# The first output projection of an encoder trunk: its attention rows read into the token operand, six of its tiles finished in the projections' PSUM banks, the last group's output moved inside SBUF

## The chip, the core and the metric

The kernel runs on one NeuronCore of a Trainium2 chip. TensorE (PE in the profile) multiplies and transposes, VectorE (DVE) and ScalarE (ACT) do the elementwise work and read PSUM, GpSimd (POOL) does a little elementwise work, and DMAs are issued from the queue of SyncE (SP), some from those of ACT and POOL. Every engine works through its own queue. The metric is the device time of one execution in microseconds (us); the median of several runs counts. A difference of 0.2% (5.4 us) is about the least that a measurement of this kernel tells from none.

## The reference

The kernel computes a two-layer encoder trunk on 1024 tokens of width 1024, in float32. Layer 0 mixes tokens with windowed attention (16 query heads of width 64 in four groups, each group with one key and value head, one sink per head) and four cross-attention heads into 256 memory tokens. Layer 1 has a gated linear recurrence in the place of the windowed attention. In both, the two kinds of heads are joined and go through one output projection, `y = concat(o, cross) @ w_out`, 1536 to 1024, which is normed and added to the stream; a gated convolutional feed-forward (FFN) follows.

```python
h = x
for layer in range(DEPTH):
    u = rmsnorm(h, norm_g[layer, 0])
    mem_kv = mem_n @ w_mem_kv[layer]
    ...
    y = mixer_window_attn(u, mem_kv, a_w_in[slot], a_sink[slot], a_w_out[slot], pos)   # layer 0
    ...
    h = h + rmsnorm(y, norm_g[layer, 1])
    f = conv_ffn(rmsnorm(h, norm_g[layer, 2]), ...)
    h = h + rmsnorm(f, norm_g[layer, 3])
```

```python
def mixer_window_attn(u, mem_kv, w_in, sink, w_out, pos):
    ...
    o = window_gqa_sink(q, k, v, sink).reshape(bsz, t, ATT_Q_W)
    return jnp.concatenate([o, memory_cross_attn(xq, mem_kv)], axis=-1) @ w_out
```

## The kernel before

Every operand of a large product is kept as two float32r halves, a high part and the rest (`split`, L85 to L87: a copy on ACT, a subtraction on DVE), and a product is three matmuls (`mm3`, L80 to L83: high by high, high by rest, rest by high). Tokens lie in eight tiles of 128. `uh` and `ul` are the two halves of the normed token operand, transposed: 128 partitions, eight blocks of features, 1024 tokens.

**Weights** come in units of 128 x 1024 through a staging pool of four buffers (`st`) and are split into a ring of four units (`wunit`, L68 to L78, with the load at L75, the copy at L76 and the subtraction at L77). The output projection's half needs six units; four go in the ring, two in a pool of its own (`xwh`, `xwl`).

**Layer 0's attention** (`window`) runs per group: `proj(g)` multiplies the eight token tiles by the group's query, key and value weights (`pj` in PSUM, two banks of the pool `psq`), rotates the result, transposes it (`ptq`, the third bank of `psq`) and splits it into `qs`, `kh` and `kl`. `attend(g, ...)` then goes over eight blocks of 128 queries: scores (`ps`, L315 and L316), maximum on DVE (L318), exponentials on ACT (L325), scaling, transposes of the probabilities (`pt`, L338), their split (`ph`, `pl`), and the products with the values (`po`, L341 and L342). Two blocks' outputs are gathered in `o` and stored to the DRAM buffer `oT[0]` by two DMAs on SP (L349). Cross-attention heads (`cross_unit`) are woven into groups 0 to 2 and stored to `oT[0]` rows 8 to 11 from ACT's queue (L224). `attend(g)` stands ahead of `proj(g + 1)` in the code; a scheduler that simulates the engines sets each engine's order, so that the projections of the next group fill the waits of the group before. After `proj(3)` the pool `psq` is released, and `attend(3)` has no projection beside it.

**The output projection of layer 0** was the class `WOut`. Its 12 feature blocks of 128 are read from `oT[0]` per token tile in three portions, blocks 0 to 5 (groups 0 to 2), 8 to 11 (cross heads) and 6 to 7 (group 3), each by a DMA on SP (L436) into a tile `or` that is then split. `wo0.open(3, 2)` does portions one and two of five tiles beside `attend(3)`: two of them end in SBUF (`part`), three stay in three banks of a new PSUM pool. `wo0.finish()` does the rest of the first 512 output columns (kept in `y0`, with sums of squares in `s0`), loads the second half's six units, and then does the second half, where all 12 blocks of each tile are read from DRAM and split again. Each tile's second half is followed by the norm, the addition to the stream (L493), the store to `h1d` and `norm_T` (L102 to L119), which norms again, transposes (L116) and writes `uh` and `ul` of that tile. `ffn` (matmuls at L638) then reads `uh` and `ul`.

**The class `Out`** already serves layer 1. It keeps no separate copy of the rows: `read` loads rows of `oT` into `ul` and splits them in place into `uh` and `ul`; `kept` multiplies straight from there; `cross` reads the four cross blocks of a tile into a small buffer; `begin` does blocks 0 to 5 of all eight tiles and copies each sum to `y0`; `finish` adds blocks 8 to 11 and 6 to 7, and does the second half from `uh` and `ul`.

In the profile `pb` is a PSUM bank of the output projection, `oh`, `ol` and `or` are its rows, `nu` is the row tile of `norm_T`, and `X`, `Y` and `V` are banks of the FFN.

Of the kernel before, what the change touches and what calls it, by code (L numbers as in the profile page):

```python
# [46 lines left out]
def build(tc, A, out):  # L47
# [179 lines left out]
    def window():  # L227
# [72 lines left out]
        def attend(g, qkv):  # L300
            qs, kh, kl, v = qkv
            for b in range(2):
                for nn in range(4):
# [42 lines left out]
                    if nn % 2 == 1:  # L346
# [16 lines left out]
        psq.release()  # L363
        ea.release()
        attend(3, cur)
        wo0.open(3, 2)
        psp.release()
        ap_.release()


    class WOut:

        groups = (range(0, 6), range(8, 12), range(6, 8))

        def __init__(self, l, src, key, order):
            self.l, self.src, self.key, self.order = l, src, key, order
            self.pools = [[], [], []]
            self.pre, self.part, self.begun, self.us = {}, {}, {}, {}
            self.psb, self.tag, self.psb2 = None, "pb", None

        def open(self, npre, nsb):

            l = self.l
            self.w1 = tc.alloc_tile_pool(name=f"wa{l}", bufs=2, reuse_waits="tile")
            if self.psb is None:
                self.psb = tc.alloc_tile_pool(name=f"wopb{l}", bufs=npre, space=PSUM, reuse_waits="tile")
            self.pools = [[self.w1] for _ in range(3)]
            if l == 0:

                self.w1.tile([P, 512], F32, tag="part", bufs=nsb, name="part")  # L390
                for g in (0, 2):
                    self.operands(g)
                for _ in range(2):
                    for x in ("xwh", "xwl"):
                        self.w1.tile([P, 1024], F32R, tag=x, name=x)
                self.operands(1)
            self.load(0)
            for t in self.order[npre:npre + nsb]:
                ps = self.bank()
                self.products(ps, t, 0)  # L400
                self.products(ps, t, 1, True)
                self.part[t] = self.w1.tile([P, 512], F32, tag="part", bufs=nsb, name="part")
                act.copy(self.part[t], ps)
            for t in self.order[:npre]:
                self.pre[t] = self.bank()
                for g in range(2):
                    self.products(self.pre[t], t, g)

        def bank(self):
            if self.psb2:  # L410
                return self.psb2.tile([P, 512], F32, tag="pb2", name="pb")
            return self.psb.tile([P, 512], F32, tag=self.tag, name="pb")

        def load(self, b, n=6):
            for i, u in enumerate((0, 1, 2, 4, 5, 3)[:n]):
                if (b, u) not in self.us:
                    self.us[b, u] = wunit(A[self.key][b, u], pl=self.w1 if i >= RING else None)
            self.b = b

        def products(self, ps, t, g, last=False, first=False, left=False):  # L420

            ks = [k for k in self.groups[g] if not (left and k in self.begun[t])]
            n = len(ks)
            oh, ol, raw = (x[:, :n, :] for x in self.operands(g))
            self.rows_of(ps, t, ks, oh, ol, raw, g == 0 or first, g == 2 or last)

        def operands(self, g):
            pl = self.pools[g][0]
            self.pools[g] = self.pools[g][1:] + self.pools[g][:1]
            m = len(self.groups[g])  # L430
            return [pl.tile([P, m, P], dt, tag=f"{x}{g}", bufs=1, name=x) for x, dt in (("oh", F32R), ("ol", F32R), ("or", F32))]
# [16 lines left out]
        def finish(self):  # L448
# [9 lines left out]
            for t in self.order:  # L458
# [4 lines left out]
                if t == self.order[5]:  # L463
                    after = self.read
# [1024 lines left out]
```

## Time and profile before

| | |
|---|---|
| median of 3 runs | 2690.17 us (2688.71 to 2694.2) |
| the profiled execution | 2686.47 us |
| its span, first to last instruction | 2684.7 us |
| TensorE clock granted, mean | 0.993 of full |
| busy: PE, DVE, ACT, POOL | 98%, 68%, 52%, 17% of the span |
| start of the FFN of layer 0 (first `X` product) | 595.20 us |

The profile is one execution. A row of the timeline gives start, duration, engine, line and operation, with the tile written and the tiles read, and in square brackets how long the engine had idled and for whom. A table of windows gives the busy time of each engine in each stretch, with instruction counts in brackets, then the clock that TensorE was granted as a share of full speed, and how busy the DMA engines were. Matmuls are pipelined, so one that lasts 0.39 us can start 0.23 us after another; the busy time of PE therefore overstates its work a little.

### The profile page before, as it was taken

To read this page: it belongs to the slowest core of one execution; us is meant where nothing else is said; L and a number is where in the kernel's file an instruction comes from. 1 tells how busy PE (TensorE), PEld (TensorE's weight loads), DVE (VectorE), ACT (ScalarE), POOL (GpSimd) and SP (SyncE) were. 2 spreads that over 40 slices of the span, in tenths; PEclk is the share of its full clock that TensorE was granted. 3 is DMA by queue.
4 is the path that set the end of the run, shared out by engine and by line. 5 is a ranking of instruction groups with operands and counts; after the bars stand their busy time and mean duration, and the time that the engine had idled before them with its cause. 6 is when DMAs were issued, how large, how long until landed. Compare 5 with 4: busy or idle time off the path is not lost.

```text
span 2684.7 us, 39333 instructions
## 1 busy us (share of the span) xinstructions
PE 2618.3 (98%) x14496; PEld 2200.0 (82%) x14496; DVE 1827.6 (68%) x3026; ACT 1384.6 (52%) x2530; POOL 469.4 (17%) x520
## 2 busy tenths in 40 slices
PE   8999999999999999999999999999999999999998
PEld 7888897788888887887888888888888788888886
DVE  6587787678656565478778686796757755656456
ACT  6367666645444445455455454545534444444453
POOL 1231110111111100032223132230211111110013
PEclk9999998999999999999999999999999999999999
DMA  7674213557877756674326252102436777774666
GB/s 281 213 166 104 60 28 117 176 183 181 216 199 200 205 165 243 191 241 157 103 84 177 76 120 70 48 29 83 150 119 178 183 202 210 198 205 160 220 196 228
DMA packets 204626, 427.00 MB, mean 159 GB/s; under 512 B 20112, under 2 KB 66576, under 8 KB 198800
## 3 DMA queue, kind: packets, MB, share of 16 engines
q1 hardware_dynamic: 171168, 326.68, 37.5%
q0 software_dynamic: 24544, 90.19, 16.1%
q10 hardware_dynamic: 8720, 7.60, 0.9%
q8 instruction: 114, 1.87, 0.3%
q14 instruction: 80, 0.66, 0.1%
HBM read 331.08 MB, written 117.44 MB: 167 GB/s over the span
## 4 chain that ended last, share of the span: by engine, by line
PE 77%; DVE 13%; ACT 4%; DMA 3%; issue 2%; POOL 1%; SPq 0%; DVEq 0%; ACTq 0%; POOLq 0%
PE X L638 27%; PE V L638 11%; PE pj L81 5%; PE pj L82 5%; PE Y L638 5%; PE pj L83 5%; PE pb L82 3%; PE pb L81 3%; PE pb L83 3%; DVE E L1194 1%; DVE ER L1229 1%; PE pt L338 1%; PE pt L116 1%; DVE wl L87 1%; PE po L1297 1%
## 5 line engine op out<-in xcount | busy, mean ns | idle before, releaser
L87 DVE TENSOR_TENSOR wl<-st,wh 128x1024 fp32r<-128x1024 f32 (+1 forms) x238 | 263.5, 1114 | 325.7 <-ACT wh L86 318.3
L86 ACT CAST wh<-st 128x1024 fp32r<-128x1024 f32 (+1 forms) x238 | 222.5, 937 | 295.2 <-PE X L638 196.2
L81 PE MATMUL pj<-uh,wh 128*128 128x512 f32 x512 | 204.1, 399 | 3.8 <-DVE xl L87 2.5
L638 PE MATMUL X<-wl,wh 128*128 128x512 f32 x528 | 204.8, 390 | 0.3 <-DVE wl L87 0.3
L638 PE MATMUL X<-wh,wl 128*128 128x512 f32 x528 | 204.6, 389 | 0.0
L82 PE MATMUL pj<-ul,wh 128*128 128x512 f32 x512 | 202.5, 396 | 0.1
L83 PE MATMUL pj<-uh,wl 128*128 128x512 f32 x512 | 201.6, 394 | 0.0
L638 PE MATMUL X<-wh 128*128 128x512 f32 x528 | 198.8, 390 | 1.7 <-DVE c L1014 0.9
L81 PE MATMUL pj<-wh,uh 128*128 128x384 f32 (+1 forms) x512 | 190.4, 372 | 4.2 <-DVE gs L1125 3.8
L82 PE MATMUL pj<-wl,uh 128*128 128x384 f32 (+1 forms) x512 | 187.3, 366 | 0.0
L83 PE MATMUL pj<-wh,ul 128*128 128x384 f32 (+1 forms) x512 | 186.8, 366 | 0.0
L77 DVE TENSOR_TENSOR wl<-st,wh 128x1024 fp32r<-128x1024 f32 (+1 forms) x92 | 119.9, 1310 | 28.1 <-ACT wh L76 27.4
L638 PE MATMUL V<-uh,wh 128*128 128x512 f32 x344 | 133.8, 389 | 0.0
L638 PE MATMUL V<-ul,wh 128*128 128x512 f32 x344 | 133.8, 389 | 0.0
L638 PE MATMUL V<-uh,wl 128*128 128x512 f32 x344 | 133.8, 389 | 0.0
L76 ACT CAST wh<-st 128x1024 fp32r<-128x1024 f32 (+1 forms) x99 | 99.9, 1015 | 50.5 <-PE pj L82 27.8
L638 PEld LDWEIGHTS X<-wh 128*128 128x128 f32 x528 | 99.1, 188 | 22.9 <-issue 1.3
L81 PEld LDWEIGHTS pj<-uh,wh 128*128 128x128 f32 x512 | 96.7, 189 | 24.2 <-DVE xl L87 2.9
L638 PEld LDWEIGHTS X<-wl,wh 128*128 128x128 f32 x528 | 99.1, 188 | 21.2 <-DVE wl L87 0.7
L638 PEld LDWEIGHTS X<-wh,wl 128*128 128x128 f32 x528 | 99.1, 188 | 20.8
L83 PEld LDWEIGHTS pj<-uh,wl 128*128 128x128 f32 x512 | 96.8, 189 | 19.2
L980 POOL TENSOR_TENSOR c<-c,g 128x512 f32<-128x512 f32 x24 | 43.4, 1828 | 393.8 <-PE X L638 162.8
(372 smaller groups left out, 7257.4 us busy)
## 6 DMA issues: line engine op xcount, KB each, us to landing
st<-hid SPq DMA_DIRECT2D x154, 256.0 KB, 3.1
st<-in_ffw_dram SPq DMA_DIRECT2D x108, 256.0 KB, 3.2
w2s<-in_ffw_dram POOLq DMA_DIRECT2D x24, 1024.0 KB, 7.9
st<-in_ffw_dram SPq DMA_DIRECT2D x46, 512.0 KB, 4.1
hid<-tt SPq DMA_DIRECT2D x88, 256.0 KB, 4.6
st<-w2s SPq DMA_DIRECT2D x88, 256.0 KB, 2.8
sx<-in_ffw_dram SPq DMA_DIRECT2D x84, 256.0 KB, 3.9
sy<-in_ffw_dram SPq DMA_DIRECT2D x42, 512.0 KB, 6.2
```

Source lines behind the costliest of these rows:

```text
L76: act.copy(h[:, :n], raw)
L77: (eng or dve).tensor_tensor(l[:, :n], raw, h[:, :n].bitcast(F32), op=ALU.subtract)
L81: pe.matmul(o, ah, bh, start=first, stop=False)
L82: pe.matmul(o, ah, bl, start=False, stop=False)
L83: pe.matmul(o, al, bh, start=False, stop=last)
L86: act.copy(h, src)
L87: dve.tensor_tensor(l, src, h.bitcast(F32), op=ALU.subtract)
L116: pe.transpose(ps[:, k, :], u[:, (4 * b + k) * P:(4 * b + k + 1) * P], ident)
L338: pe.transpose(tp[:, j, :], sm[:, j, c * P:(c + 1) * P], ident)
L638: pe.matmul(o, x, y, start=new, stop=e, skip_group_check=not first)
L980: pool.tensor_tensor(y[q][:, t, :], y[q][:, t, :], g3[:, c], op=ALU.mult)
L1194: dve.tensor_tensor_scan(B[:, rev], smask, a_[:, rev], 0.0, op0=ALU.mult, op1=ALU.add)
```

## The change

Layer 0's output projection uses `Out`, and `WOut` is gone. Seven things follow.

- `psq`, the three banks of the projections, is no longer released before `attend(3)`; `begin` uses its two `pj` banks and its `ptq` bank in turn.
- `begin` reads blocks 0 to 5 of each of the eight token tiles from `oT[0]` into `ul` with one DMA on SP per tile and splits them in place. A tile can be read when the store of group 2's rows has landed and the last product of `proj(3)` that reads those blocks of the tile is done. Tiles 0 and 1 have high priority.
- The first 18 matmuls of each of the eight tiles (blocks 0 to 5) then run, and ACT copies each sum to `y0`.
- In `finish` the first six tiles take the same three banks, and only tiles 6 and 7 and the second half use three more (`late`).
- For group 3, `o` goes by two DMAs on SP from SBUF to `ul`, and is split there. It is not stored to DRAM and not read back.
- The second half reads only the four cross blocks of each tile from DRAM; the other eight are taken from `uh` and `ul`.
- `y0` lies in the pool of the projection and is allocated before the last group ends.

```diff
@@ attend
-                    if nn % 2 == 1:
+                    if nn % 2 == 1 and g == 3:
+                        ts_ = slice((n - 1) * P, (n + 1) * P)
+                        oh, ol = uh[:, 6:8, ts_], ul[:, 6:8, ts_]
+                        for hp in range(2):
+                            nc.sync.dma_start(ul[hp * 64:(hp + 1) * 64, 6:8, ts_].bitcast(F32), o[:, hp::2, :])
+                        act.copy(oh, ol.bitcast(F32))
+                        dve.tensor_tensor(ol, ol.bitcast(F32), oh.bitcast(F32), op=ALU.subtract)
+                    elif nn % 2 == 1:
@@ window
-        psq.release()
         ea.release()
         attend(3, cur)
-        wo0.open(3, 2)
+        wo0.open()
+        y0 = wo0.w1.tile([P, NT, 512], F32, bufs=1, name="y0")
+        wo0.begin(psq, ("pj", "pj", "ptq"), [y0[:, t, :] for t in range(NT)])
         psp.release()
         ap_.release()
-    class WOut:
...
@@ Out.finish
-            self.banks += [(psb2, "pb2", n)] * n
+            late = [(psb2, "pb2", n)] * n
             y0 = self.y0
             s0 = wp.tile([P, NT], F32, bufs=1, name="s0")
-            for t in self.order:
+            for i, t in enumerate(self.order):
+                if i == (6, 0)[l]:
+                    self.banks += late
+                    self.used = (3, 0)[l]
                 ps = self.bank()
@@ build
-    wo0 = WOut(0, A["x"], "wout0", list(range(NT)))
+    wo0 = Out(0, A["x"], "wout0", list(range(NT)))
```

The functions of `Out` that layer 0 now calls, unchanged:

```python
def read(self, ks, c0, c1, eng):
    c = (slice(None), slice(ks[0], ks[-1] + 1), slice(c0, c1))
    raw = ul[c].bitcast(F32)
    eng.dma_start(raw, oT[self.l][ks[0]:ks[-1] + 1, :, c0:c1].rearrange("k p t -> p k t"))
    act.copy(uh[c], raw)
    dve.tensor_tensor(ul[c], raw, uh[c].bitcast(F32), op=ALU.subtract)

def begin(self, psb, tags, y0):
    ...
    for i, t in enumerate(self.order):
        if i < 2:
            with tc.high_priority(AHEAD):
                self.read(self.groups[0], t * P, (t + 1) * P, eng)
        else:
            self.read(self.groups[0], t * P, (t + 1) * P, eng)
        ps = self.bank()
        self.kept(ps, t, self.groups[0], True, True)
        act.copy(y0[t], ps)
    self.used = 0
```

How the change moves instructions shows in the order in which they stand on each engine; x2 behind a row stands for two alike in a row. First PE at the start of the last group's attention. Before, the first two products of the output projection (`pb_5277`, from `oh_5278`) stand behind scores of the group's fourth block (`ps_4875`, `ps_4879`).

```order
L315 MATMUL ps_4875<-kh_4328,qs_4472 128x384
L315 MATMUL ps_4879<-kh_4328,qs_4473 128x384
L342 MATMUL po_4699<-pl_4717,v_4330 128x512
L338 MATMUL pt_4771<-ident_74,sm_4724 128x128 x4
L316 MATMUL ps_4875<-kl_4329,qs_4472 128x384
L316 MATMUL ps_4879<-kl_4329,qs_4473 128x384
L81 MATMUL pb_5277<-wh_5241,oh_5278 128x512
L82 MATMUL pb_5277<-wl_5242,oh_5278 128x512
```

After, the first ones (`pb_5271`, straight from `uh` and `ul`) stand behind the last products of the third cross-attention head (`po_4188`, `pt_4289` is the fourth head's transposed probabilities).

```order
L83 MATMUL po_4188<-ph_4194,kvl_4118 128x512
L81 MATMUL po_4188<-ph_4206,kvh_4117 128x512
L82 MATMUL po_4188<-pl_4207,kvh_4117 128x512
L83 MATMUL po_4188<-ph_4206,kvl_4118 128x512
L217 MATMUL pt_4289<-ident_74,xp_4245 128x128 x4
L81 MATMUL pb_5271<-wh_5231,uh_78 128x512
L82 MATMUL pb_5271<-wl_5232,uh_78 128x512
L83 MATMUL pb_5271<-wh_5231,ul_79 128x512
```

So 36 products, those of tiles 0 and 1, move from the middle of the attention to the place ahead of it.

PE at the end of the last group's attention. Before, behind the last four products with the values (`po_5194`) stand six of one tile's cross rows (`pb_5560`), and then `pb_5576`.

```order
L341 MATMUL po_5194<-ph_5200,v_4330 128x512
L342 MATMUL po_5194<-pl_5201,v_4330 128x512
L341 MATMUL po_5194<-ph_5211,v_4330 128x512
L342 MATMUL po_5194<-pl_5212,v_4330 128x512
L81 MATMUL pb_5560<-xwh_5271,oh_5561 128x512
L82 MATMUL pb_5560<-xwl_5272,oh_5561 128x512
L83 MATMUL pb_5560<-xwh_5271,ol_5562 128x512
L81 MATMUL pb_5560<-xwh_5271,oh_5561 128x512
L82 MATMUL pb_5560<-xwl_5272,oh_5561 128x512
L83 MATMUL pb_5560<-xwh_5271,ol_5562 128x512
L81 MATMUL pb_5576<-xwh_5271,oh_5577 128x512
L82 MATMUL pb_5576<-xwl_5272,oh_5577 128x512
```

After, 18 products of tile 0's second half (`pb_5895`, from `uh` and `ul`) stand there, eight of tile 1's (`pb_5974`) behind them.

```order
L341 MATMUL po_5199<-ph_5205,v_4330 128x512
L342 MATMUL po_5199<-pl_5206,v_4330 128x512
L341 MATMUL po_5199<-ph_5216,v_4330 128x512
L342 MATMUL po_5199<-pl_5217,v_4330 128x512
L81 MATMUL pb_5895<-wh_5691,uh_78 128x512
L82 MATMUL pb_5895<-wl_5692,uh_78 128x512
L83 MATMUL pb_5895<-wh_5691,ul_79 128x512
L81 MATMUL pb_5895<-wh_5691,uh_78 128x512
```

The second half begins there, ahead of the first half's end, and the first product that reads group 3's rows stands 40 products behind the last `po`.

SP's queue ahead of the last group's attention. Before, three pairs of stores of group 2's rows (L349) stand together, the weight loads (L75) behind them, and the first read of rows (`or_5280`) last.

```order
L349 DMA oT0_57<-o_3504 64x2x256 x2
L349 DMA oT0_57<-o_3837 64x2x256 x2
L349 DMA oT0_57<-o_3982 64x2x256 x2
L75 DMA st_5267<-in_wout0_dram 128x1024
L75 DMA st_5273<-in_wout0_dram 128x1024
L75 DMA st_5776<-in_wout0_dram 128x1024
L75 DMA st_5782<-in_wout0_dram 128x1024
L436 DMA or_5280<-oT0_57 128x6x128
```

After, the reads of rows into `ul_79` (L401) stand two by two between the stores, which are L356 now.

```order
L401 DMA ul_79<-oT0_57 128x6x128 x2
L356 DMA oT0_57<-o_3504 64x2x256 x2
L401 DMA ul_79<-oT0_57 128x6x128 x2
L356 DMA oT0_57<-o_3837 64x2x256 x2
L401 DMA ul_79<-oT0_57 128x6x128 x2
L75 DMA st_5257<-in_wout0_dram 128x1024
L75 DMA st_5263<-in_wout0_dram 128x1024
L356 DMA oT0_57<-o_3982 64x2x256 x2
L75 DMA st_5693<-in_wout0_dram 128x1024
L401 DMA ul_79<-oT0_57 128x6x128 x2
```

The last pair of stores (`o_3982`) has moved behind a pair of reads and two weight loads, and the reads of tiles 6 and 7 stand behind it.

ACT's queue at the same place. Before, it goes from the copies of projection and cross-attention results (`v_4330`, `xo_4301`, `qs_4637`) to the first exponentials (L325) of group 3.

```order
L279 CAST v_4330<-pj_4598 128x64
L223 COPY xo_4301<-po_4276 128x512
L294 CAST qs_4637<-ptq_4632 64x512
L224 DMA oT0_57<-xo_4301 128x512
L296 CAST qs_4638<-ptq_4632 64x512
L325 ACTIVATE sm_4664,su_4668<-sm_4664,nm_4666 128x256 x4
```

After, the casts of tiles 6 and 7's rows (`uh_78` from `ul_79`, L402) stand among them.

```order
L279 CAST v_4330<-pj_4598 128x64
L402 CAST uh_78<-ul_79 128x6x128
L294 CAST qs_4637<-ptq_4632 64x512
L402 CAST uh_78<-ul_79 128x6x128
L223 COPY xo_4301<-po_4276 128x512
L325 ACTIVATE sm_4663,su_4667<-sm_4663,nm_4665 128x256 x4
```

The first exponentials stand behind both casts. The six casts of tiles 0 to 5 stand further ahead, among the copies of `proj(3)`; on DVE the eight subtractions (L403) stand in the same way, those of tiles 6 and 7 right behind the maximum of group 3's first block.

117 lines of the change are left out of this document (removed).

## The prediction

> **What bounds the kernel now.** I read the page's totals first, then busy time by stretch around the last group's attention, then PE's waits there.
>
> ```profile
> span 2684.7 us, 39333 instructions
> PE 2618.3 (98%) x14496; PEld 2200.0 (82%) x14496; DVE 1827.6 (68%) x3026; ACT 1384.6 (52%) x2530; POOL 469.4 (17%) x520
> ```
>
> PE carries the time, and the change neither adds nor removes a matmul. So it can win only time in which PE does less than it could, or lose by making PE wait where it does not. The profiled execution took 2686.47 us, 1.8 above its span and 3.7 below the median of the runs; I take a difference worked out on the span over to the median as it is. A difference under 0.2% (5.4 us) is what a measurement of this kernel can't tell from none.
>
> A row of the next table has a stretch's length, the busy time of PE, PEld, DVE, ACT and POOL, the granted clock, the DMA engines' share and GB/s.
>
> ```profile
> 360.00:400.00 40.00, 39.65 (x252) 37.92 (x251) 31.33 (x86) 28.08 (x78) 4.68 (x8) 1.00 0.05 14
> 400.00:410.00 10.00, 8.05 (x46) 6.41 (x45) 9.88 (x21) 6.06 (x10) 4.10 (x4) 0.99 0.72 213
> 410.00:420.00 10.00, 8.56 (x28) 6.24 (x28) 9.19 (x34) 8.49 (x28) 0.00 (x0) 0.50 0.47 141
> 420.00:430.00 10.00, 8.19 (x28) 5.77 (x28) 8.06 (x17) 9.69 (x20) 0.00 (x0) 0.65 0.24 69
> 430.00:480.00 50.00, 50.00 (x254) 42.27 (x253) 33.40 (x90) 31.50 (x78) 0.00 (x0) 1.00 0.35 98
> 480.00:490.00 10.00, 9.21 (x50) 7.34 (x50) 6.96 (x14) 6.48 (x15) 0.00 (x0) 1.00 0.29 73
> 490.00:500.00 10.00, 6.74 (x31) 5.05 (x30) 4.22 (x7) 5.10 (x11) 0.00 (x0) 1.00 0.37 97
> 540.00:590.00 50.00, 50.00 (x246) 41.94 (x245) 38.73 (x69) 26.71 (x53) 6.04 (x11) 1.00 0.58 184
> 590.00:600.00 10.00, 9.01 (x44) 7.18 (x44) 8.11 (x15) 4.20 (x8) 1.65 (x3) 1.00 0.50 179
> ```
>
> Three places are short of work: the start of group 3's attention (400 to 430), its tail (480 to 500) and the end of the norm (590 to 600). Counting busy time times clock as work, 400 to 430 lost 10 - 8.05 x 0.99 = 2.0, 10 - 8.56 x 0.50 = 5.7 and 10 - 8.19 x 0.65 = 4.7, together 12.4 us; 480 to 500 lost 0.8 + 3.3 = 4.1, the norm's end 1.0. The ceiling is about 17.5 us. A product that moves into these stretches saves its length; one that moves elsewhere saves nothing.
>
> **The start: 36 products moved ahead.** The maxima on DVE and the exponentials on ACT hold PE up, and no product of the projection is ready.
>
> ```profile
> PE ps L315 <- DVE mx L318: 2.8, 4, 1.2
> 410.69 0.61 DVE L318 CUSTOM_DVE_ANT_0 sm<-ps,wmask,sk 128x384 f32<-128x384 f32 x1
> 411.22 0.51 ACT L325 ACTIVATE sm<-sm,nm 128x256 f32<-128x256 f32 x1
> 417.56 1.91 PE L338 MATMUL pt<-ident,sm 128*128 128x128 f32 x8
> 426.95 0.39 PE L81 MATMUL pb<-wh,oh 128*128 128x512 f32 x1
> 429.61 0.50 PE L83 MATMUL pb<-wh,ol 128*128 128x512 f32 x1 [0.26 <-DVE ol L87]
> 607.42 2.72 PE X L638 x12
> ```
>
> The first row is a group of waits (sum, count, longest). The last, from the chain, gives a 128x512 product at full clock: 2.72 / 12 = 0.227 us. Before, the first product of the output projection ran at 426.95, and from 429.61 they ran without waits. Now 36 stand ahead of the attention; two had run before 429.61 in any case, so 34 x 0.227 = 7.7 us of work moves from the full stretch into the hole.
>
> Against it stands that on ACT the first exponentials, and on DVE the second block's maximum, now wait behind the reads of tiles 6 and 7. Their chain by rows:
>
> ```profile
> 398.69 1.23 SPq L349 DMA_DIRECT2D oT<-o  x2
> 403.65 0.33 SPq L75 DMA_DIRECT2D st<-in_wout_dram  x1
> 409.28 0.39 SPq L436 DMA_DIRECT2D or<-oT  x1
> oT<-o SPq DMA_DIRECT2D x12, 128.0 KB, 2.4
> or<-oT SPq DMA_DIRECT2D x16, 384.0 KB, 3.7
> DMA to landing us min/median/max: 2.1/3.4/8.5
> 425.69 0.84 ACT L86 CAST oh<-or 128x768 fp32r<-128x768 f32 x1
> 537.10 0.95 DVE L87 TENSOR_TENSOR ol<-or,oh 128x768 fp32r<-128x768 f32 x1
> ```
>
> The last store of group 2 went at 398.69 before. It now stands behind two weight loads, the second of which went at 403.65, so it goes at 404.0; its second half, 0.6 later, lands 2.4 after that, at 407.0. The two reads follow, 0.39 apart, and land 3.7 later, at 410.7 and 411.1. Two casts of 0.84 end at 412.4, the subtractions of 0.95 at 413.4. The exponentials start at about 413, 1.8 later than 411.22. Of that 0.84 comes back, since the cast at 425.69 is out of the way by then, but the second maximum is delayed by more than the first exponentials; I take 1.4 for the start of the dense run. Four score products of some 0.17 that were done by then are not: 0.7. Net 7.7 - 1.4 - 0.7 = **5.6 us gained**. Bounds: reads that land after 8.5 instead of 3.7 take 4.8 of it and leave about 1; with the clock at full, what can be won rises to 12.4 less these 2.1, about 10. I take 5.6, as the median landing is that of the same shape.
>
> The clock stood at 0.50 and 0.65 although none of the waits for a maximum was longer than 1.2 us. The Trainium skill, "TensorE: Matmul & The Clock Gate", section "HAM oscillation — how this bites in real kernels", says that gaps of PE under some 3.4 us keep the clock up; by that rule only waits were lost here, and with the same products moved the sum would be the same. The trace disagrees, and the measurement decides.
>
> **The tail.**
>
> ```profile
> 482.03 0.50 PE L341 MATMUL po<-ph,v 128*128 128x512 f32 x1 [0.34 <-DVE o L345]
> 486.84 0.50 PE L81 MATMUL pb<-xwh,oh 128*128 128x512 f32 x1 [0.44 <-ACT oh L86]
> 491.04 0.40 ACT L86 CAST oh<-or 128x256 fp32r<-128x256 f32 x1 [0.58 <-DMA or<-oT]
> 491.46 0.58 ACT L344 COPY o<-po 64x512 f32<-64x512 f32 x1
> 492.08 0.68 DVE L345 TENSOR_TENSOR o<-po,o 64x512 f32<-64x512 f32 x1 [0.18 <-ACT o L344]
> 492.82 0.50 PE L341 MATMUL po<-ph,v 128*128 128x512 f32 x1 [2.09 <-DVE o L345]
> 496.58 0.50 PE L81 MATMUL pb<-xwh,oh 128*128 128x512 f32 x1 [1.17 <-ACT oh L86]
> ```
>
> The square brackets say how long PE stood and for whom: 0.34 + 0.44 + 2.09 + 1.17 = 4.0 us. The two waits for `oh` (1.6) go, since the products there now read rows that have long been split. The two for `o` (a bank of `po` that must be emptied) stay in part: the cast of read rows at 491.04, 0.40, no longer stands ahead of the copy of `o`, and eight products stand ahead of the last block where six did, 2 x 0.227; I take 0.9. **2.5 us gained**, between 0 (other waits take their place) and 4.0. Group 3's rows no longer go to DRAM and back: after `o`'s 0.58 and 0.68 come two issues (1.23, as at 398.69), 2.4 to land, a cast like that copy (0.58) and a subtraction (0.68), 6.2 us. The 40 products that stand ahead of the first one that needs them cover 40 x 0.227 = 9.1. If that cover were gone, the whole 6.2 would show. The casts wait for these moves in ACT's and DVE's queues, and behind the last of them there is nothing urgent but `y`. Behind the last moves on SP stand gains of the norm and rows of the stream, wanted some 40 us later, and the reads of the second half.
>
> **The end of the norm.**
>
> ```profile
> 594.38 1.06 PE L116 MATMUL pt<-ident,nu 128*128 128x128 f32 x8 [0.99 <-DVE nu L112]
> 595.20 0.48 PE L638 MATMUL X<-uh,xwh 128*128 128x512 f32 x1
> ```
>
> PE waited 0.99 for the last tile's norm. Now 24 products of `X` and 24 of `Y`, 10.9 us, stand ahead of the last two tiles' transposes. **1.0 gained**, between 0 and 1.0.
>
> **Six more reads in group 2's attention.** The casts and subtractions of tiles 0 to 5 move into the stretch before 400, where PE was busy for 39.65 of 40. They bring 6 x 0.84 = 5.0 to ACT's 28.08 and 6 x 0.95 = 5.7 to DVE's 31.33, which is then at 37 of 40, as busy as in 410 to 420, where PE did 8.56 of 10. Bounds 0 and 4 x (10 - 8.56) = 5.8 us. I take a quarter, **1.4 lost**: the products of `proj(3)`, which need neither engine, stand there to fill waits.
>
> **At nothing.** The second half reads 4 of 12 blocks again where it read 12; PE is busy for 50.00 of 50 between 540 and 590, so fewer reads there free DMA, ACT and DVE but no time. The weights of the second half are split earlier, beside the attention, where DVE had 33.40 of 50. Eight copies to `y0` take the place of two to `part` and six to `y0`. The three banks of `late` are free long before tile 6 wants them.
>
> Sum: 5.6 + 2.5 + 1.0 - 1.4 = 7.7 us; 2690.2 - 7.7 = **2682.5** (the profiled execution 2678.8).
>
> **The rivals.**
>
> Slower, by the queues (R1). The reads of tiles 0 to 5 wait for a store, a product of `proj(3)` and a landing; their casts stand in ACT's queue ahead of the copies that empty `pj`. If the landing isn't covered, PE stops.
>
> ```profile
> 408.80 0.59 ACT L223 COPY xo<-po 128x512 f32<-128x512 f32 x1 [2.27 <-DMA oT<-xo]
> 409.29 0.58 ACT L294 CAST qs<-ptq 64x512 fp32r<-64x512 f32 x1
> ```
>
> Here ACT stood 2.27 us for a DMA with a cast of `qs` behind it. The Trainium skill, "PSUM — Partial Sum Buffer", section "Engine vs sequencer instructions", says that the queues of ScalarE and VectorE are strictly in order; this trace agrees. Price: 3.7 for the landing less 0.4 for one instruction ahead, 3.3 x 6 = 20 us against gains of 9.1: slower by 11, 2701. It decides from (9.1 + 5.4) / 6 = 2.4 us per read on PE's path. Against it: two `pj` banks and the attention's products stand between.
>
> No difference (R2). Between 400 and 420 DVE was busy for 9.88 and 9.19 of 10. If it sets the pace, two more subtractions and late landings push all of group 3 back: the start yields its lower bound, 1, the tail the 1.6, the norm 1.0, less 1.4: 2.2, or 2688.
>
> More (R3). The 36 products stand in one row before the hole and could keep the clock at full. The start then reaches half way to its upper bound (+2.2), the tail all of its 4.0 (+1.5), the reads cost nothing (+1.4): 12.8, or 2677.4. The Trainium skill, "TensorE: Matmul & The Clock Gate", section "What's actually happening", has the clock return after a busy stretch of some 3.4 us, which speaks for it; whether it would stay there no run here shows.
>
> That the change doesn't do what it says is settled by the order: ahead of the attention's last `po`, 270 products of the projection stand where 168 did.
>
> **Chances.** My forecast 0.50, with its own range 2677 to 2687, of which four parts in five lie below 2684.8; R3 0.16; R2 0.16; R1 0.18, as the queues' waits are what the trace of before shows least. Faster: 0.40 + 0.16 = 0.56; same: 0.10 + 0.16 = 0.26; slower: 0.18. The range, 2673 to 2692, reaches past R3 by the rest of the ceiling and past R2 by as much as a run's spread; it leaves out most of R1 and little below.
>
> **What would show it.** Right: PE near full and the clock near 1.00 in the first part of 400 to 430, the first exponentials near 413, no waits for `oh` at the tail, the first `X` product 7.7 us earlier than its 595.20. Wrong: PE waits of over 2 us for copies of `pj` (L279) or a lower PE share before 400 (R1); first exponentials after 416 or a clock that stays at 0.5 until 430 (R2).

## The result, and the profile after

The changed kernel takes 2678.70 us (median of 5 runs, 2677.03 to 2679.18), the kernel before beside it 2690.74 (2688.71 to 2694.2): a ratio of 0.9953, 95% interval 0.9939 to 0.9968, or 12 us. The profiled execution took 2679.18 us with a span of 2677.4.

The page's totals of the changed kernel, and the table of stretches with the columns that were explained above:

```profile
span 2677.4 us, 39198 instructions
...
PE 2614.8 (98%) x14496; PEld 2198.1 (82%) x14496; DVE 1817.4 (68%) x3012; ACT 1374.8 (51%) x2510; POOL 476.8 (18%) x520
```

```profile
360.00:400.00 40.00, 39.05 (x241) 36.82 (x242) 33.65 (x91) 29.03 (x78) 3.45 (x6) 1.00 0.19 54
400.00:410.00 10.00, 9.09 (x56) 8.04 (x55) 8.99 (x15) 7.97 (x12) 4.26 (x4) 1.00 0.55 134
410.00:420.00 10.00, 10.00 (x48) 8.20 (x46) 6.61 (x16) 4.83 (x13) 2.39 (x2) 1.00 0.74 234
420.00:430.00 10.00, 8.09 (x35) 5.95 (x34) 9.07 (x29) 7.41 (x19) 0.00 (x0) 0.83 0.27 79
430.00:480.00 50.00, 49.76 (x247) 42.09 (x247) 34.92 (x91) 37.32 (x88) 0.00 (x0) 1.00 0.23 69
480.00:490.00 10.00, 10.00 (x54) 8.39 (x53) 5.66 (x15) 4.73 (x8) 0.00 (x0) 1.00 0.39 105
490.00:500.00 10.00, 10.00 (x53) 8.26 (x52) 6.60 (x15) 5.79 (x17) 0.00 (x0) 1.00 0.10 29
580.00:590.00 10.00, 9.06 (x44) 7.32 (x43) 7.75 (x14) 3.97 (x9) 2.27 (x3) 1.00 0.48 163
```

Between 410 and 420, where PE stood at half clock, it is now full at clock 1.00. Of the hole at the start there remains 420 to 430, at 0.83. The tail at 480 to 500 is full. Two things got worse: 360 to 400 has lost 0.6 us of PE, and the end of the norm still has its gap, now at 580 to 590.

Busy time overstates PE's work, so the comparisons below use a finer count. The time between the starts of successive matmuls, less what the first of them takes at full clock when they run back to back (0.227 us for 512 columns, 0.174 for 384, 0.116 for 256, 0.109 for a transpose), is called *lost*, and is summed over a stretch of the trace. It holds waits and low clock together. A row is good to some tenths of a microsecond; the expectations below go by a coarser count of the same kind, up to 0.5 lower. The second traces are further executions of the same two kernels.

| lost by PE, us | 340 to 400 | 400 to 440 | 440 to 480 | 480 to 520 | 520 to 610 | together |
|---|---|---|---|---|---|---|
| before | 2.1 | 15.0 | 0.5 | 5.3 | 1.5 | 24.3 |
| before, second trace | 2.2 | 15.3 | 0.5 | 5.3 | 1.4 | 24.7 |
| changed | 5.2 | 7.2 | 0.5 | 1.2 | 1.7 | 15.7 |
| changed, second trace | 5.3 | 7.6 | 0.5 | 1.3 | 1.6 | 16.2 |

So the start gave 7.8 us (forecast 5.6), the tail 4.1 (2.5), the norm's end nothing (1.0), and the last group but one cost 3.1 (1.4): together 8.6 by the first traces and 8.5 by the second, where the forecast had 7.7. The rest of the 12 lies behind this part of the kernel, and is the subject of the last experiments.

Times in a trace count from its first instruction, and executions stand up to 3.8 us apart before this part begins. The first rotation of group 3's projection on POOL (L276) tells by how much; where the text counts from there, it says "from the rotation".

| us from the first instruction | that rotation | first exponentials of group 3 | first `X` product |
|---|---|---|---|
| before | 345.25 | 411.22 | 595.20 |
| changed | 345.13 | 417.90 | 585.35 |
| without the 36 products ahead | 343.78 | 416.49 | 591.99 |
| before, hole filled | 346.50 | 414.43 | 600.85 |
| group 3's rows through DRAM | 343.54 | 416.21 | 589.00 |
| weight loads behind the store | 347.33 | 415.82 | 587.40 |
| splits of six tiles left out | 346.50 | 414.75 | 585.34 |
| splits of tiles 2 to 7 behind | 345.17 | 414.36 | 588.74 |
| last tile's bank | 343.77 | 416.48 | 582.87 |

In the changed kernel one more tile's transposes stand behind the first `X` product, 0.9 us; the same instructions of the feed-forward come 9.0 us earlier than before.

The start of group 3's attention in the changed kernel:

```profile
406.35 0.67 DVE L345 TENSOR_TENSOR o<-po,o 64x512 f32<-64x512 f32 x1
407.05 1.23 SPq L356 DMA_DIRECT2D oT<-o  x2
410.15 1.26 SPq L401 DMA_DIRECT2D ul<-oT  x2
415.05 0.83 ACT L402 CAST uh<-ul 128x768 fp32r<-128x768 f32 x1 [4.71 <-DMA ul<-oT]
417.90 0.51 ACT L325 ACTIVATE sm<-sm,nm 128x256 f32<-128x256 f32 x1
421.46 0.63 PE L286 MATMUL ptq<-ident,rq 128*128 128x128 f32 x4 [1.34 <-DVE qs L297]
421.54 0.62 DVE L318 CUSTOM_DVE_ANT_0 sm<-ps,wmask,sk 128x384 f32<-128x384 f32 x1
431.05 0.39 PE L81 MATMUL pb<-wh,uh 128*128 128x512 f32 x1
```

The last store of group 2 went at 407.05, right behind group 2's last output (L345), and not at 404.0. The reads went at 410.15, and ACT stood 4.71 us for the landing. In the chain of work that ended last, this landing is one step:

```profile
410.64 6.03 DMA ul<-oT
```

So it took 6.0 us where the forecast had 3.7. The first exponentials came at 417.90, five later than forecast, and the next block's maximum at 421.54. Yet the products run on from 431.05, as forecast: the 36 products covered most of this wait.

### The profile page after: what moved, and what is told of

Its sections match the earlier page's. It is cut to its first block, busy times and chain, and to the rows that moved or that the text cites. A ratio compares the mean times of both kernels' runs of the same rounds, so it can differ in the third digit from the quotient of the medians.

```text
span 2677.4 us, 39198 instructions
## 1 busy us (share of the span) xinstructions
PE 2614.8 (98%) x14496; PEld 2198.1 (82%) x14496; DVE 1817.4 (68%) x3012; ACT 1374.8 (51%) x2510; POOL 476.8 (18%) x520
## 3 DMA queue, kind: packets, MB, share of 16 engines
q0 software_dynamic: 24544, 90.19, 16.2%
## 4 chain that ended last, share of the span: by engine, by line
PE 76%; DVE 13%; DMA 4%; ACT 3%; issue 2%; POOL 1%; SPq 0%; ACTq 0%; DVEq 0%; POOLq 0%
PE X L508 27%; PE V L508 11%; PE pj L81 5%; PE Y L508 5%; PE pj L82 5%; PE pj L83 5%; PE pb L82 3%; PE pb L81 3%; PE pb L83 3%; DVE E L1064 1%; PE pt L338 1%; DVE ER L1099 1%; DVE wl L87 1%; DVE wl L77 1%; PE pt L116 1%
```

## The experiments

Each kernel ran beside the kernel before on the same chip. Where an expectation names the changed kernel, 2678.7 is meant; a second set of runs of it gave 2678.47 (2677.98 to 2679.98).

**Without the 36 products ahead.** In layer 0, all products of the first part stand behind the first block's products with the values (`mark['pe']` is the last of these).

```diff
-                self.kept(ps, t, self.groups[0], True, True)
+                if self.l == 0:
+                    with tc.issue_after(mark['pe'].ins):
+                        self.kept(ps, t, self.groups[0], True, True)
...
```

> The changed kernel, but the products of the projection stand behind the first block's products with the values, as they did before the change; the reads stay where they are. Theory (the 36 products fill the hole at the start): their 7 to 8 us come back, 2685 to 2688, with PE at about 14 us lost between 400 and 440 and the granted clock at 0.5 to 0.7 there again. Rival (the gain is the tail's, the start is bound by the maxima and exponentials whatever stands ahead): 2678 to 2681.

Measured: 2691.02 us (2684.68 to 2692.60), ratio 1.0000 (0.9991 to 1.0009). All of the gain is gone, which is more than the theory's 7 to 8. The trace is that of the fastest of the eleven executions.

```profile
410.00:420.00 10.00, 7.35 (x23) 5.27 (x24) 9.24 (x29) 5.83 (x15) 1.26 (x2) 0.61 0.78 257
420.00:430.00 10.00, 7.74 (x28) 5.89 (x27) 7.86 (x23) 9.93 (x28) 0.00 (x0) 0.71 0.12 31
```

The hole is back at clocks of 0.61 and 0.71, and 400 to 440 loses 14.9 us, 7.7 more than in the changed kernel. The tail keeps its gain (0.4 lost in 480 to 520, against 5.3 before), but 340 to 400 loses 5.2 as in the changed kernel, and 520 to 610 loses 4.1 against 1.5:

```profile
591.99 0.50 PE L514 MATMUL X<-uh,xwh 128*128 128x512 f32 x1 [2.04 <-DVE y L494]
...
594.22 0.63 PE L514 MATMUL X<-ul,xwh 128*128 128x512 f32 x1
594.65 0.63 PE L514 MATMUL X<-uh,xwl 128*128 128x512 f32 x1
```

The first `X` waits longer here for the bank that `y` has to leave, and behind that wait products start 0.43 us apart instead of 0.227. Against before, 4.9 are won and 3.1 and 2.6 lost: without the 36 products the other parts of the change come to nothing. Against the changed kernel these stretches give 9.3 of the 12.3 us: 7.7 is the hole, as the theory has it, and 2.4 is the wait at the end, which the edit brought with it, less 0.8 won at the tail.

**Filling the hole of the kernel before with other products.**

```diff
+        for r in range(2):
+            ps = psq.tile([P, 384], F32, tag="pj", bufs=2, name="pj")
+            for k in range(24):
+                pe.matmul(ps, uh[:, k % KT, :P], ul[:, (k + 1) % KT, :384], start=k == 0, stop=k == 23)
         psq.release()
```

> The kernel before, with 48 extra products of 128x384 (48 x 0.174 = 8.4 us of PE at full clock) that need nothing but the token operand, ahead of the last group's attention; their result is used nowhere. Theory (the hole is empty of work, and the products that fill it cost nothing of their own): within 2 us of before, 2689 to 2693. If half of the loss there is the low clock and a filled PE keeps the clock up: 3 to 5 us faster than before, 2685.5 to 2688. Rival (the time at the start is PE's own at a low clock, so that extra products add to it): 8 us slower, 2699.

Measured: 2696.95 us, ratio 1.0027 (1.0018 to 1.0036): 7.3 slower, near the rival.

```profile
410.00:420.00 10.00, 9.96 (x61) 9.11 (x59) 6.07 (x21) 6.16 (x17) 0.00 (x0) 1.00 0.51 164
420.00:430.00 10.00, 5.94 (x20) 2.90 (x19) 9.50 (x24) 8.29 (x23) 0.00 (x0) 0.92 0.03 13
...
414.43 0.51 ACT L325 ACTIVATE sm<-sm,nm 128x256 f32<-128x256 f32 x1
```

The clock did come up, to 1.00 and 0.92, and still the hole was not free. 400 to 440 lost 10.2 instead of 15.0, so 4.8 of the 8.4 us were hidden and 3.6 were paid there. From the rotation, the extra products push the first exponentials by 2.0 us (67.9 for 66.0), and the hole moves behind them with the group's own chain of maxima, exponentials and transposes. From the rotation, the feed-forward began 4.4 us later than before (254.4 for 250.0); the rest of the 7.3 lies in the later stages. So the rival's reason (PE's own time at a low clock) is not what this shows either: with the clock up, PE still waits for the chain. In the changed kernel the exponentials are late too, and it wins because its products are work that otherwise stands behind.

**Group 3's rows through DRAM again.**

```diff
-                    if nn % 2 == 1 and g == 3:
+                    if nn % 2 == 1 and g == 4:
...
+                if l == 0:
+                    self.read(self.groups[2], t * P, (t + 1) * P, nc.sync)
                 self.cross(ps, t, True, False)
```

> The changed kernel, with group 3's rows stored to DRAM and read back tile by tile. Theory (40 products of 0.227 = 9.1 us stand ahead of the first that needs them; store and read back take 0.58 + 0.68 + 1.23 + 2.4 + 0.39 + 2.5 + 0.4 + 0.43 = 8.6): nothing to 1 us slower than the changed kernel, 2678 to 2680. Rival (the move inside SBUF is what took the tail's waits away): the tail's 4 to 5 us come back, 2683 to 2684.

Measured: 2681.24 us (2680.55 to 2682.76), ratio 0.9965 (0.9953 to 0.9978): 2.5 to 2.8 slower than the changed kernel, between the two expectations.

```profile
489.87 0.50 PE L81 MATMUL pb<-xwh,uh 128*128 128x512 f32 x1 [1.27 <-ACT uh L402]
...
507.09 0.50 PE L81 MATMUL pb<-xwh,uh 128*128 128x512 f32 x1 [1.61 <-ACT uh L402]
```

The waits for rows read back return, and 480 to 520 loses 6.1 where the changed kernel loses 1.2; behind the second wait, products start 0.43 us apart until 511. In the changed kernel one wait for the moved rows is left:

```profile
504.34 0.62 ACT L351 CAST uh<-ul 128x512 fp32r<-128x512 f32 x1 [0.62 <-DMA ul<-o]
505.01 0.50 PE L81 MATMUL pb<-xwh,uh 128*128 128x512 f32 x1 [0.55 <-ACT uh L351]
509.26 0.39 PE L342 MATMUL po<-pl,v 128*128 128x512 f32 x1
510.30 0.68 DVE L345 TENSOR_TENSOR o<-po,o 64x512 f32<-64x512 f32 x1 [0.72 <-ACT o L344]
514.14 0.62 ACT L351 CAST uh<-ul 128x512 fp32r<-128x512 f32 x1 [3.87 <-DMA ul<-o]
514.79 0.69 DVE L352 TENSOR_TENSOR ul<-ul,uh 128x512 fp32r<-128x512 f32 x1 [3.81 <-ACT uh L351]
518.56 0.39 PE L81 MATMUL pb<-xwh,uh 128*128 128x512 f32 x1
```

The rows that PE waits for at 505.01 are those of the third pair of blocks, whose first reader stands ahead of the last block's products with the values (509.26). The last pair's rows, for which the 40 products were counted, are split by 515.5, 5.8 us behind the end of the last product with the values, and first read at 518.56: that cover was long enough, with 3 us to spare. So it is in this experiment: the two waits belong to the second and the third pair, and the last pair costs none, as the theory has it. What the theory left out are the earlier pairs, which have less cover. By the medians the move inside SBUF is worth 2.5 to 2.8 us, most of what the tail gained.

**The weight loads behind the last store.**

```diff
-            self.load(0, self.w1)
+            if self.l == 0:
+                self.load(0, self.w1, 1)
+                with tc.issue_after(mark['sp'].ins):
+                    self.load(0, self.w1)
...
```

> The changed kernel, with the weight loads of the projection behind the last store of group 2 on SP instead of ahead of it. The reads of tiles 6 and 7, issued at 410.15 in the changed kernel, then go some 6 to 8 us earlier, and the first exponentials, at 417.9, start at 411 to 412. Theory (the late landing costs the start what the forecast's lower bound says, up to 4.8): 2 to 5 us faster than the changed kernel, 2674 to 2677. Rival (the 36 products cover the wait, and later weights cost as much): 2678 to 2680.

Measured: 2677.59 us (2676.96 to 2679.28), ratio 0.9952 (0.9939 to 0.9964): not to be told from the changed kernel.

```profile
407.68 1.23 SPq L356 DMA_DIRECT2D oT<-o  x2
409.01 1.97 SPq L75 DMA_DIRECT2D st<-in_wout_dram  x4
411.15 1.07 SPq L403 DMA_DIRECT2D ul<-oT  x2
415.82 0.50 ACT L325 ACTIVATE sm<-sm,nm 128x256 f32<-128x256 f32 x1
```

From the rotation, the store went 1.6 us earlier and the reads 1.2, not 6 to 8. The store does not wait for the loads ahead of it, but for group 2's last output, which comes at 406.35 in the changed kernel and came 8 us earlier before:

```profile
397.98 0.68 DVE L345 TENSOR_TENSOR o<-po,o 64x512 f32<-64x512 f32 x1 [0.53 <-ACT o L344]
```

Yet from the rotation the first exponentials came 4.3 us earlier than in the changed kernel (68.5 for 72.8), because the casts of tiles 6 and 7 now stand behind them, so the edit does tell what the late exponentials cost. 400 to 440 loses 5.7 instead of 7.2, 480 to 520 loses 2.5 instead of 1.2, and the feed-forward begins as far from the rotation as in the changed kernel (240.1 and 240.2). So the rival is nearer: the 36 products cover most of the wait, and what little the earlier exponentials give is lost again at the tail.

**The casts and subtractions of six tiles left out.** The rows of tiles 0 to 5 are read, but not split.

```diff
+            if self.l == 0 and c0 < 6 * P:
+                return
             act.copy(uh[c], raw)
             dve.tensor_tensor(ul[c], raw, uh[c].bitcast(F32), op=ALU.subtract)
```

> The changed kernel without the casts and subtractions of tiles 0 to 5 (their rows are loaded into the operand, but not split). Theory (casts and subtractions on ACT and DVE are what costs the last group but one its time, 4.7 us lost between 340 and 400 against 2.0 before): the 2.8 us come back there, the stretch loses 2 to 2.5, and the whole is 2 to 4 us faster than the changed kernel, 2674.5 to 2676.5. Rival (the loss there is the order's or the transfers'): 4 to 5 us lost there as before, 2677.5 to 2679.

Measured: 2676.5 us (2674.99 to 2680.74), ratio 0.9949 (0.9936 to 0.9963), which four runs can't tell from the changed kernel. 340 to 400 loses 2.1, as before the change: the theory's place is right. But 480 to 520 loses 2.9, so of the 3.1 us saved ahead 1.7 are lost again at the tail; from the rotation, the feed-forward begins 1.4 us earlier than in the changed kernel (238.8 for 240.2).

What the splits do there is seen around 357. The changed kernel, with the rotation's addition on POOL, the subtraction of tile 1's rows on DVE, and the transposes of the rotated rows on PE:

```profile
356.91 1.95 POOL L276 TENSOR_TENSOR rq<-t,t 128x320 f32<-128x320 f32 x1 [10.63 <-DVE t L275]
...
357.20 0.94 DVE L403 TENSOR_TENSOR ul<-ul,uh 128x768 fp32r<-128x768 f32 x1
...
358.92 0.33 PE L286 MATMUL ptq<-ident,rq 128*128 128x128 f32 x1 [0.97 <-POOL rq L276]
```

The same addition before, and in the kernel without the splits:

```profile
356.70 0.86 POOL L276 TENSOR_TENSOR rq<-t,t 128x320 f32<-128x320 f32 x1 [10.30 <-DVE t L275]
```

```profile
358.01 0.86 POOL L276 TENSOR_TENSOR rq<-t,t 128x320 f32<-128x320 f32 x1 [10.37 <-DVE t L275]
```

Beside the subtraction the addition takes 1.95 us instead of 0.86, 1.09 more, and PE waits 0.97 for it. The Trainium skill, "SBUF — State Buffer", section "Who interferes with whom", says that a VectorE instruction with two inputs in SBUF and a GpSimd instruction that reads SBUF exclude each other at a shared port; the trace agrees, in that the added 1.09 is about the subtraction's 0.94. It was the addition, begun 0.29 us ahead, that took longer; the subtraction took no more than that shape takes elsewhere (0.95 in the kernel before). The other losses between 340 and 400 are waits of 0.3 to 0.5 for `pl`, which stands behind the subtractions on DVE.

**The splits of tiles 2 to 7 behind the first exponentials.** The edit names the whole reads and the last of these exponentials (`mark['act']`); in the run only the casts and subtractions moved.

```diff
+                elif self.l == 0 and i >= 2:
+                    with tc.issue_after(mark['act'].ins):
+                        self.read(self.groups[0], t * P, (t + 1) * P, eng)
```

> The changed kernel with the reads of tiles 2 to 7 behind the exponentials of group 3's first block; tiles 0 and 1 stay where they are. Theory (reads ahead cost 2.8 us before 400, and those of tiles 6 and 7 hold the first exponentials back from 411 to 418): the first exponentials at 411 to 414, but six casts and subtractions (5.0 and 5.7 us) then lie in the hole; net 0 to 3 us faster than the changed kernel, 2675.5 to 2679. Rival (in the hole ACT and DVE set the pace, so that work there costs all its length): 2 to 6 us slower, 2681 to 2685.

Measured: 2681.69 us (2680.96 to 2682.03), ratio 0.9965 (0.9953 to 0.9978): 3 slower than the changed kernel, the rival.

```profile
356.97 1.96 POOL L276 TENSOR_TENSOR rq<-t,t 128x320 f32<-128x320 f32 x1 [10.66 <-DVE t L275]
```

The transfers of tiles 2 to 5 still went before 400, by SP's queue; only tiles 0 and 1 are split there, and the loss is 5.2, the same as with six. So the cost ahead is not so much per read, nor is it the transfers': the first two splits make all of it, 1.1 of the 3.1 by the clash at 357. The four splits of tiles 2 to 5 cost nothing that shows where they were; in the hole they cost, 8.8 against 7.2 in 400 to 440 and 3.0 against 1.2 in 480 to 520. The first exponentials come at 414.36, 3.5 us earlier than in the changed kernel, and the whole is slower all the same.

**The last tile's bank.**

```diff
+            self.used += 1 if l == 0 else 0
             for t in self.order:
                 pool.tensor_tensor(y0[t], y0[t], g1[:, :512], op=ALU.mult)
```

> The changed kernel with the second half's banks taken one further on, so that the last tile does not use the bank that the first product of X gets. Theory (the first X waits 0.94 us for the last tile's y to leave its bank): that wait goes, 0.5 to 1 us faster, 2677.7 to 2678.2. Rival (the wait passes to another bank or to the norm): 2678.4 to 2679.

Measured: 2678.07 us (2676.15 to 2678.52), ratio 0.9953 (0.9940 to 0.9967). The first product of `X` in the changed kernel, and here:

```profile
585.35 0.50 PE L508 MATMUL X<-uh,xwh 128*128 128x512 f32 x1 [0.94 <-DVE y L488]
```

```profile
582.87 0.48 PE L509 MATMUL X<-uh,xwh 128*128 128x512 f32 x1
```

The wait is gone and went nowhere else: 520 to 610 loses 0.5 instead of 1.7. (Of the 2.5 us between the two starts, 1.4 stood at the rotation already.) In the time, half a microsecond is within the spread.

**A third tile in the hole.** The first four tiles take `pj`'s two banks in turn, and their sums are copied out with priority (with the edit of the last tile's bank).

```diff
-                ps = self.bank()
+                tg = "pj pj pj pj ptq pj pj ptq".split()[i] if self.l == 0 else None
+                ps = self.bank() if tg is None else psb.tile([P, 512], F32, tag=tg, bufs=tags.count(tg), name="pb")
...
```

> The changed kernel with the second half's banks one further on, and with the first four tiles of the projection taking the two banks of pj in turn, their sums copied out early, so that a third tile's products are ready in the hole between 420 and 431, where the changed kernel loses 4.2 us. Theory (the hole lacks work): 1 to 3 us faster than the changed kernel, 2675.5 to 2677.5. Rival (the hole is the attention's own chain, and the products stand in order behind it): 2677.5 to 2679.

Measured: 2678.37 us (2676.45 to 2680.25), ratio 0.9961 (0.9947 to 0.9974): the rival. 400 to 440 loses 6.9, and the tail 2.6 instead of 1.2. The third tile's products still stand behind the hole on PE; the first of them runs at 430.83.

**Both small edits together**, the loads behind the store and the last tile's bank:

> The changed kernel with the two edits that gained a little by themselves: the weight loads behind the last store, and the second half's banks one further on. Theory (they act in different places, at the start and at the end of the norm): 1.1 + 0.6 = 1.7 us faster than the changed kernel, 2676.5 to 2677.2. Rival (the first one's gain was chance in the later stages, since its feed-forward began no earlier): 2677.5 to 2678.7.

Measured: 2678.01 us (2674.59 to 2680.2), ratio 0.9962 (0.9949 to 0.9976). No version tried can be told from the changed kernel on the fast side.

**Where the other 3 us come from.** Two runs of the unchanged kernels, for more traces, and one with a delay ahead of the feed-forward.

> The kernel before, once more, for a second trace. The first trace is of an execution of 2686.5 us, 4 us under the median of its runs, while the changed kernel's runs lie within 2 us of each other. Theory (the clock in the hole at the start varies from run to run, and that is where the runs differ): if this execution is slower than 2688, the stretch 400 to 440 loses 2 us or more beyond the first trace's 14.9, at a lower clock. Rival (the spread comes from layer 1, alike in both kernels): the loss at 400 to 440 is 14 to 16 us whatever the time.

Measured: 2693.36 us, one run. 400 to 440 lost 15.3 against 15.0, and the feed-forward began at 595.96 against 595.20. The theory falls: 0.8 of the 6.9 us between the two traces lies ahead of the feed-forward. Compared by the starts of the same instructions on DVE, 3.2 come at one place near 1052, 2 near 1567 and some 2 between 1850 and 1950, and 1.1 are made up near the end. The first of them, in the first trace and in the second:

```profile
1051.04 0.63 ACT L661 ACTIVATE wh<-st 128x512 fp32r<-128x512 f32 x1 [2.62 <-DMA st<-w2s]
1052.20 0.50 PE L638 MATMUL X<-wh 128*128 128x512 f32 x1 [0.76 <-ACT c L1011]
```

```profile
1053.56 0.63 ACT L661 ACTIVATE wh<-st 128x512 fp32r<-128x512 f32 x1 [4.14 <-DMA st<-w2s]
1054.72 0.50 PE L638 MATMUL X<-wh 128*128 128x512 f32 x1 [2.53 <-ACT c L1011]
...
1056.87 0.63 PE L638 MATMUL X<-wh 128*128 128x512 f32 x1
1057.30 0.63 PE L638 MATMUL X<-wl,wh 128*128 128x512 f32 x1
```

PE waits for a copy out of `X` (`c`), and this copy stands on ACT behind the split of a weight (`wh`) that had not landed. The longer wait makes 1.8 of the 3.2 us. The rest is clock: behind it products start 0.43 us apart for 3.3 us, where behind the shorter wait they do not.

> The changed kernel once more, beside the two others of this call: 2677 to 2680. If its runs lie within 2.5 us of each other again while those of before spread over 6 or more, the spread belongs to the kernel and not to the chip.

Measured: 2678.47 us, five runs within 2.0, beside runs of before from 2684.6 to 2694.9. So on one chip the two kernels spread differently, and the spread is not the chip's alone.

```diff
+            if l == 0:
+                ps = self.psb.tile([P, 512], F32, tag="ptq", bufs=1, name="pb")
+                for k in range(40):
+                    pe.matmul(ps, uh[:, k % KT, :P], ul[:, (k + 1) % KT, :512], start=k == 0, stop=k == 39)
             psp.release()
```

> The changed kernel with 40 extra products (40 x 0.227 = 9.1 us) right ahead of the feed-forward; their result is used nowhere. In traces, the changed kernel begins the feed-forward 9 us earlier than before, but its median is 12 us lower. Theory (the other 3 us are chance stalls in the later stages that have nothing to do with the change): 9.1 less the 0.9 of the wait that they cover, 2686 to 2688, runs within 3 us of each other. Rival (the stalls later depend on when the feed-forward begins against the transfers): 2690 to 2692, runs spread over 6 us or more as those of before.

Measured: 2686.90 us (2683.57 to 2689.26), ratio 0.9988 (0.9979 to 0.9997): 8.4 slower than the changed kernel beside it, as the theory has it, with a spread of 5.7, which is the rival's. So when the feed-forward begins may have a part in the spread, but not in the median as far as these runs go. The narrow spread does not come with the change as such either: two kernels that differ from the changed one by small edits far ahead, the one without six splits and the one with both small edits, spread over 5.7 and 5.6 us. In traces, the feed-forward's instructions from 600 on come 9.0 (first traces) and 8.9 us (second) earlier in the changed kernel; against the median of before the gain was 12.0 in the first runs and 10.6 in those beside this. Near 1052 the stall is a weight that lands late; why such stalls cost the changed kernel less stays open.

## Why the prediction was right, and where its steps were not

The time fell into the range and into the forecast's own range (2677 to 2687), 3.8 us below its 2682.5. That it came so near is in part luck. Four terms were off, by 2.2, 1.6, 1.0 and 1.7 us, the first two one way and the last two the other, and some 3 us came from the later stages, for which the sum had no term.

- **What bounds the kernel.** Right: PE, short of work at three places. The tail was filled, the hole at the start by half, the end of the norm not.
- **The start.** The mechanism is shown: without the 36 products the hole is back, and the gain with it. The term was 5.6 and measured 7.8. Its chain was too early at each step: the store waits for group 2's last output, not for the weight loads ("it goes at 404.0"; 407.05), the landing took 6.0 us instead of 3.7, the exponentials came at 417.90 instead of 413. That is past the 416 which the prediction names as a sign of R2, and yet the start gave more than forecast: the exponentials' time was not the measure. Where they came 3.5 to 4.5 us earlier (loads behind the store, splits left out, splits behind), 400 to 440 lost 1.5 less, the same and 1.6 more. What made the term too small is not shown. The clock would fit, which the sum left as it was: between 410 and 430, clocks of 0.50 and 0.65 are worth 10 x 0.50 + 10 x 0.35 = 8.5 us less than the full one, those of 1.00 and 0.83 only 1.7 less. With the tail's 4.1, these are the sizes that R3 had (7.8 and 4.0); its third, reads that cost nothing, is the one that was wrong.
- **The tail.** Mis-sized: 2.5 forecast, 4.1 measured. That the two waits for `o` "stay in part" failed; they went too, as the profile after has no wait for `o` between 480 and 520. The 6.2 us for the last move were right (5.8), and its 9.1 of cover was enough. That "40 products that stand ahead of the first one that needs them" are the cover holds for the last pair of blocks alone, though: a product that reads the third pair's rows stands ahead of the last block, and waited 0.55. That the move is worth most of the tail's gain was seen only by undoing it.
- **The end of the norm.** Failed: 1.0 forecast, nothing measured. The wait of 0.99 for `nu` was replaced by one of 0.94 for the bank that `y` had to leave. The step asked what covers the transposes, and did not ask whose bank `X` takes.
- **Six more reads.** The sign was right and the size half: 1.4 forecast, 3.1 measured. Neither was it the six splits' sum of work, as the bounds were built, but the first two, by one clash of DVE with POOL and a few waits in DVE's queue. "The products of `proj(3)`, which need neither engine, stand there to fill waits" overlooked the transposes of `proj(3)`, which wait for POOL. R1's mechanism, queues that hold others up, exists at 3 of its price of 20.
- **At nothing.** 540 to 580 was full in both kernels, so the saved reads bought nothing, as said.
- **R2.** Not the outcome, but its reason shows in part: the group's own chain decides what is left of the hole, as the filled hole of the kernel before and the splits behind the exponentials tell.

## What to carry to other kernels

Where an attention's first block holds PE up, products that would run later anyway are the ones to put ahead of it: 34 products of 7.7 us gained 7.8 there, while 8.4 us of products that add work made the kernel 7.3 slower. Before moving splits beside another stage, look for what POOL does at that place: here a DVE subtraction with both inputs in SBUF more than doubled a POOL addition on which PE waited (1.95 us for 0.86). And where work at the end of a stage is covered by the next stage's products, check which bank those products take, and who leaves it last.

## What was not expected of the hardware

The granted clock fell to 0.50 and 0.65 in stretches where PE was busy for 82 to 86% of the time by its records and no wait was longer than 1.2 us; in the changed kernel it was 1.00 while the 36 products ran and 0.83 behind them, with a wait of 1.34. Single waits in otherwise full stretches show no one length at which it falls: behind waits of 1.61, 2.04 and 2.53 us (507.09, 591.99 and 1054.72 in three runs above) products started 0.43 us apart for about 3.3 us, while behind one of 2.09 (492.82 in the kernel before) they did not, and the clock from 490 to 500 was 1.00.

The kernel before spreads over 10 us from run to run (2684.6 to 2694.9), the changed one over 2 in each of its two sets, though the two traces of before differ by stalls hundreds of microseconds behind the changed part.
